# Expert gather that fills a whole PSUM bank before copying it, and larger limits on the ring of expert weights

## The chip, the core and the metric

The kernel runs on one NeuronCore of one Trainium2 chip. The core has a matrix engine (TensorE, "PE" in the profile), three engines for elementwise work (VectorE "DVE", ScalarE "ACT", GpSimd "POOL") and a queue, SyncE ("SP"), which here issues the loads from HBM. Each engine works through its own list of instructions in order and waits on semaphores where it needs something from another. The metric is device time in microseconds for one launch.

## The reference

Two layers over 512 tokens of width 1024, all float32. Each layer adds three things to the residual x:

```python
x = x + merged @ w_out[i]                 # merged = sig(ga) * attention + sig(gb) * convolution
x = x + _hier_moe(_rms_norm(x, norm_ffn[i]), ...)   # top-1 group, top-2 of its 8 experts
x = x + sigmoid(_rms_norm(x) @ W_pg) * (p[i] @ W_pe)
```

There are 32 experts. Each has a gate and an up matrix (1024 x 512) and a down matrix (512 x 1024), and computes `(silu(xb @ w_gate) * (xb @ w_up)) @ w_down` for its tokens. The weights of the experts of one layer are 384 pieces of 512 KB, some 200 MB, and each of them is read from HBM once.

## The kernel before

**Layer.** The first part of a layer, the mixer, projects x, runs attention and convolution, and then works through eight chunks `ao0` to `ao7` (attention and convolution output, 24 matmuls each; the loop that ends at L746) and eight chunks `wo0` to `wo7` (output projection, the routing of tokens woven into its second half). The weights of a mixer chunk arrive raw (L207, 512 KB, issued by SP), ACT rounds them to a high part (L225), POOL makes the low part (L230), and PE multiplies with both.

**MoE.** The second part handles the experts in eight chunks c = 0 to 7 of four experts (two pairs). In each chunk PE goes, in this order, through: gate and up matmuls of both pairs; the down matmuls of the pairs of the chunk before; transposes of the hidden values (`ps_hT`); the gather for the next chunk (`ps_xg`); and the combine of the pairs whose down is ready (`ps_c`, added to x by DVE at L1079). PE's instructions are kept in program order in the MoE.

**Gather.** The tokens of an expert are picked by matmul with a one-hot matrix: for each of eight slices of 128 features there are eight matmuls of 128x256 (four token tiles, high and low part, `gather_part`), and ACT copies the result with a scale (L998) to `s_xg`. A slice fills half of a PSUM bank, and so two slices share one bank, four banks per gather.

**Weights.** `pump` (L241) issues the expert weights in a fixed order through SP into slots of the pool `s4`, 45 tiles of 4 KB per partition, which also holds other large tiles (raw mixer weights, `s_xg`, `s_yh`, x). A call stops when the pool has fewer than `keep` free tiles, or when the ring already holds `limit` weights. The limits `RING` apply in the mixer: RING[0] in the loop over `ao`, RING[1] behind it and in `wo0` to `wo3`, RING[2] in the routing part. In the MoE only `KEEP[c]` counts. SP is one queue in order: a load whose slot isn't free yet holds up all loads behind it. At most eight loads are in flight.

**Around the middle.** At the start of chunk 4 the inputs of the embeddings are loaded (L1109, split by ACT at L1110 and by POOL at L1111), and two raw loads (L207) follow on SP. After chunk 4 stands a loop for experts with too many tokens (L1218). It normally runs zero times, but all engines meet there, and each waits for the loads issued so far.

Of the kernel before, what the change touches and what calls it, by code (L numbers as in the profile page):

```python
# [12 lines left out]
AF = mybir.ActivationFunctionType  # L13
# [14 lines left out]
GS = 256  # L28
# [25 lines left out]
              + [f"wo{i}" for i in range(8)] + ["pe0", "pe1"] + [f"pg{i}" for i in range(8)])  # L54
NCH = len(SEQ_CHUNKS)

RING = 2, 12, 20
KEEP = 6, 10, 6, 6, 8, 10, 12, 8
LAGS = 1, 2, 1, 5
OVC = 4  # L60
# [95 lines left out]
class Trunk:  # L156
# [310 lines left out]
    def mixer(self, l):  # L467
        nc = self.nc
        v, act = nc.vector, nc.scalar
# [254 lines left out]
        for j in range(8):  # L724
            c = pos[f"ao{j}"]
            wh, wl = self.take(c)
            pab = [self.ps.get(F32, "ya"), self.ps.get(F32, "yb")]
            for s, src in ((1, cv), (0, oT)):
                for k in range(4):
                    w = slice((4 * s + k) * P, (4 * s + k + 1) * P)  # L730
                    self.mm3(pab[s], wh[:, w], wl[:, w], src[0](k), src[1](k), k == 0, k == 3)
            self.done(c)
            g = gates.pop(0)
            ga, gb = g[:, :T], g[:, T:]
            act.activation(pab[1], pab[1], AF.Identity, bias=self.smt[:, S_BO + j:S_BO + j + 1])
            v.scalar_tensor_tensor(gb, gb, 1.0, pab[1], op0=OP.add, op1=OP.mult)
            v.scalar_tensor_tensor(pab[0], ga, 1.0, pab[0], op0=OP.add, op1=OP.mult)
            v.tensor_tensor(pab[0], pab[0], gb, op=OP.add)
            for h in range(2):
                a = slice(256 * h, 256 * h + 256)  # L740
                act.activation(mT[0].half(j, h), pab[0][:, a], AF.Copy, scale=0.5)
                v.scalar_tensor_tensor(mT[1].half(j, h), pab[0][:, a], 0.5, mT[0].half(j, h).bitcast(F32),
                                       op0=OP.mult, op1=OP.subtract)
            self.ps.free(2)
            self.s4.free()
            self.pump(RING[0])  # L746
        for s in oT + tuple(cv):
            s.free()
        self.pump(RING[1])


        pacc = [self.ps.get(F32, "wo") for _ in range(NT)]
        for i in range(4):
            self.step_b(pos[f"wo{i}"], pacc, mT, 2 * i, i == 0, i == 3)
            self.pump(RING[1])
        for t in range(NT):
# [9 lines left out]

        def hook():
            self.advance(steps)
            self.pump(RING[2])
        for t in range(NT):  # L770
            steps.append(self.route_tile(t))
            self.half[t] = self.token_b(cs, mT, t, hook)
            if t % 2:
                for s in mT:
                    s.free(t // 2)
# [189 lines left out]
    def moe(self, l):  # L965
        nc = self.nc
        self.nc = Engines(self.tc, ("te",))
        v, act, pe = nc.vector, nc.scalar, self.nc.tensor
        oh = self.oh0
# [12 lines left out]
        def gather(oh, xg, h):  # L982

            scale = lambda k: self.smt[:, S_NF + k:S_NF + k + 1]
            out = lambda k: xg[h // 2][:, (k % 4) * GS:(k % 4 + 1) * GS]
            if self.xg0:
                for k in (2 * h, 2 * h + 1):
                    ps = self.xg0.pop(0)[:, :GS]
                    self.gather_part(ps, oh, k, NT - 1)
                    self.last_a = act.activation(out(k), ps, AF.Copy, scale=scale(k)).ins  # L990
                    self.ps.free()
                return
            ps = self.ps.get(F32, "xg")
            for i in range(2):
                k, w = 2 * h + i, slice(i * GS, (i + 1) * GS)
                for t in range(NT):
                    self.gather_part(ps[:, w], oh, k, t)
                act.activation(out(k), ps[:, w], AF.Copy, scale=scale(k))  # L998
            self.ps.free()

        oht, gs, rh, hT, ys = {}, {}, {}, {}, {}
# [121 lines left out]
        for h in range(4):  # L1123
            gather(oh, xg, h)
        self.s4.free()
        for c in range(NC2):
# [4 lines left out]
            if c < NC2 - 1:  # L1131
                oh = self.onehots(c + 1)
# [19 lines left out]
            if c < NC2 - 1:  # L1152
                xg = [self.s4.get(F32, "xg") for _ in range(2)]
                for h in range(4):
                    gather(oh, xg, h)
                self.s4.free()
                if c == NC2 - 2:
                    self.s4.free(2 * NT)
# [324 lines left out]
```

## Time and profile before

| | us |
|---|---|
| median of 3 runs | 1946.11 (1943.98 to 1948.0) |
| profiled execution | 1943.51 |
| its span | 1941.7 |
| PE busy | 1812.1 (93%) |
| DVE, ACT, POOL busy | 916.9, 565.8, 377.9 |

The granted clock of TensorE was 0.974 of full speed over the span. In the profile a wait is written `[idle before <-releaser]`; `SPq` and `DVEq` are the sequencers of SyncE and VectorE. The section on rows below has what was read.

### The profile page before, as it was taken

The page shows a single profiled execution, that of the slowest core. Times are in us where ns is not written, and L with a number is a line of the kernel's source. Part 1 is how long each engine was busy: PE and PEld are TensorE (multiplying, and loading weights), DVE is VectorE, ACT ScalarE, POOL GpSimd, SP SyncE. Part 2 cuts the span into 40 slices and gives each one's busy share as a digit, 9 for nine tenths or more (in the row PEclk, how much of TensorE's full clock was granted, in tenths as well). Part 3 has the DMA queues.
Part 4 walks back from the last instruction along what each step waited for, and adds up shares of the span by engine and source line. Part 5 has one row for each costly group of instructions (what it writes and reads, how often), then busy time and mean ns, then how long its engine had stood idle before and what let it go on. Part 6 is the DMA issues. An engine that isn't in the chain of part 4 may idle for free. (4 is left out here: it accounts for less than half of the span.)

```text
span 1941.7 us, 23302 instructions
## 1 busy us (share of the span) xinstructions
PE 1812.1 (93%) x8532; PEld 1124.4 (58%) x8532; DVE 916.9 (47%) x2165; ACT 565.8 (29%) x1071; POOL 377.9 (19%) x201
## 2 busy tenths in 40 slices
PE   5999999999999889999989999998999989999987
PEld 4776777753454345354767776877444553454456
DVE  5677754652431332323657777537432423332146
ACT  4444444220111012112634555333110111021045
POOL 3444324201000000000444444241010000000021
PEclk9999999999989999999999999999999999999999
DMA  5211227589999889997231112375898989899941
GB/s 217 83 55 66 65 98 227 189 321 357 349 351 410 343 312 382 388 409 303 81 117 65 61 59 66 127 242 195 308 401 326 381 351 401 349 364 409 409 176 44
DMA packets 133319, 478.59 MB, mean 246 GB/s; under 512 B 14800, under 2 KB 15312, under 8 KB 133200
## 3 DMA queue, kind: packets, MB, share of 16 engines
q1 hardware_dynamic: 133200, 477.04, 65.1%
q8 instruction: 70, 1.15, 0.2%
q14 instruction: 49, 0.40, 0.1%
HBM read 474.89 MB, written 2.10 MB: 246 GB/s over the span
## 5 line engine op out<-in xcount | busy, mean ns | idle before, releaser
L230 POOL TENSOR_TENSOR s_lo<-s_raw,s_hi 128x1024 fp32r<-128x1024 f32 x114 | 272.3, 2400 | 950.5 <-ACT s_hi L225 326.6
L94 PE MATMUL ps_g<-s_w,s_xg 128*64 128x512 f32 x1024 | 230.9, 604 | 4.4 <-DVEq L1218 4.4
L94 PE MATMUL ps_y<-s_w,s_hT 128*64 128x512 f32 x1024 | 225.8, 593 | 0.4 <-DMA s_w<-wdn 0.4
L94 PE MATMUL ps_u<-s_w,s_xg 128*64 128x512 f32 x1024 | 225.2, 592 | 0.0
L290 PE MATMUL ps_z<-s_hTl,s_hi 128*128 128x512 f32 x512 | 204.4, 399 | 0.0
L289 PE MATMUL ps_z<-s_hTh,s_hi 128*128 128x512 f32 x512 | 202.0, 395 | 0.0
L291 PE MATMUL ps_z<-s_hTh,s_lo 128*128 128x512 f32 x512 | 200.4, 391 | 0.0
L94 PE MATMUL ps_xg<-s_OH,s_xh 128*128 128x256 f32 x476 | 138.9, 322 | 59.6 <-ACT s_xg L998 55.8
L1079 DVE TENSOR_TENSOR s_x<-s_x,ps_c 128x512 f32<-128x512 f32 x128 | 87.9, 687 | 155.6 <-PE ps_c L94 132.4
L94 PEld LDWEIGHTS ps_y<-s_w,s_hT 128*64 128x64 f32 x1024 | 74.5, 137 | 148.4 <-issue 136.2
L94 PEld LDWEIGHTS ps_g<-s_w,s_xg 128*64 128x64 f32 x1024 | 73.0, 139 | 149.7 <-issue 142.2
L94 PEld LDWEIGHTS ps_u<-s_w,s_xg 128*64 128x64 f32 x1024 | 73.4, 137 | 146.3 <-issue 141.2
L501 DVE SCALAR_TENSOR_TENSOR s_acc<-ps_z,smt,s_acc 128x511 f32<-128x511 f32 (+27 forms) x210 | 153.7, 732 | 4.2
L94 PEld LDWEIGHTS ps_xg<-s_OH,s_xh 128*128 128x128 f32 x476 | 101.4, 213 | 74.2 <-ACT s_xg L998 68.5
L94 PE MATMUL ps_xg<-s_OH,s_xl 128*128 128x256 f32 x476 | 130.9, 305 | 0.0
L225 ACT ACTIVATE s_hi<-s_raw 128x1024 fp32r<-128x1024 f32 x120 | 124.5, 1055 | 0.7
L1034 ACT ACTIVATE s_h<-ps_g,rs 128x512 f32<-128x512 f32 x32 | 22.0, 687 | 343.1 <-PE ps_g L94 331.8
L1035 DVE SCALAR_TENSOR_TENSOR s_h<-s_h,ps_g 128x512 f32<-128x512 f32 x32 | 22.0, 687 | 188.2 <-ACT s_h L1034 188.2
L290 PEld LDWEIGHTS ps_z<-s_hTl,s_hi 128*128 128x128 f32 x512 | 96.7, 189 | 21.4 <-issue 3.0
L289 PEld LDWEIGHTS ps_z<-s_hTh,s_hi 128*128 128x128 f32 x512 | 96.5, 189 | 21.5 <-issue 1.0
L291 PEld LDWEIGHTS ps_z<-s_hTh,s_lo 128*128 128x128 f32 x512 | 96.5, 189 | 19.1
L1045 ACT ACTIVATE s_hT<-ps_hT 128x512 f32<-128x512 f32 x32 | 17.6, 596 | 304.1 <-PE ps_hT L94 263.2
(256 smaller groups left out, 2873.9 us busy)
## 6 DMA issues: line engine op xcount, KB each, us to landing
s_w<-wu SPq DMA_DIRECT2D x256, 512.0 KB, 10.1
s_w<-wdn SPq DMA_DIRECT2D x256, 512.0 KB, 10.2
s_w<-wg SPq DMA_DIRECT2D x248, 512.0 KB, 10.2
s_raw<-wd SPq DMA_DIRECT2D x124, 512.0 KB, 3.5
s_w<-wg SPq DMA_DIRECT2D x16, 256.0 KB, 7.9
s_x<-x SPq DMA_DIRECT2D x4, 512.0 KB, 9.4
out<-s_n SPq DMA_DIRECT2D x8, 256.0 KB, 2.0
s_gain<-gains SPq DMA_DIRECT2D x3, 512.0 KB, 3.7
```

The source lines that it names most:

```text
L94: i = f(*a, **k)
L225: nc.scalar.activation(hi, raw, AF.Copy)
L230: nc.gpsimd.tensor_tensor(lo, raw, hi.bitcast(F32), op=OP.subtract)
L289: mm(out, lh, rh, start=start, stop=False)
L290: mm(out, lh, rl, start=False, stop=False)
L291: mm(out, ll, rh, start=False, stop=stop)
L501: v.scalar_tensor_tensor(o, i, w, o, op0=OP.mult, op1=OP.add)
L1034: act.activation(t, pg, AF.Tanh, scale=rh[p])
L1035: v.scalar_tensor_tensor(t, t, 1.0, pg, op0=OP.add, op1=OP.mult)
L1045: act.activation(o, ps, AF.Copy)
L1079: v.tensor_add(xs, xs, ps)
```

## The change

In `gather`, the eight matmuls of both halves of a bank are written first, and the two copies after them. Before, each half had its eight matmuls and then its copy. The limits of the ring become 6, 18, 28 in place of 2, 12, 20; in the loop over `ao` the limit now grows by one with each chunk; in the routing part three tiles of the pool are kept free. The kernel has one line more after it, so that lines behind the gather are counted one higher.

```diff
-RING = 2, 12, 20
+RING = 6, 18, 28
...
-            self.pump(RING[0])
+            self.pump(RING[0] + j)
...
-            self.pump(RING[2])
+            self.pump(RING[2], keep=3)
...
             ps = self.ps.get(F32, "xg")
+            half = [ps[:, i * GS:(i + 1) * GS] for i in range(2)]
             for i in range(2):
-                k, w = 2 * h + i, slice(i * GS, (i + 1) * GS)
                 for t in range(NT):
-                    self.gather_part(ps[:, w], oh, k, t)
-                act.activation(out(k), ps[:, w], AF.Copy, scale=scale(k))
+                    self.gather_part(half[i], oh, 2 * h + i, t)
+            for i in range(2):
+                act.activation(out(2 * h + i), half[i], AF.Copy, scale=scale(2 * h + i))
             self.ps.free()
```

**PE, in a gather of layer 0.** `s_OH` is the one-hot matrix, `s_xh` and `s_xl` are the high and low parts of the tokens; the two halves of bank `ps_xg_3551` follow each other. Before:

```order
1609 L94 MATMUL ps_xg_3551<-s_OH_3276,s_xh_2809 128x256 [waits PE_49]
1610 L94 MATMUL ps_xg_3551<-s_OH_3276,s_xl_2810 128x256
...
1616 L94 MATMUL ps_xg_3551<-s_OH_3276,s_xl_3115 128x256
1617 L94 MATMUL ps_xg_3551<-s_OH_3276,s_xh_2809 128x256 [waits Activation_49]
1618 L94 MATMUL ps_xg_3551<-s_OH_3276,s_xl_2810 128x256
```

Now:

```order
1609 L94 MATMUL ps_xg_3551<-s_OH_3276,s_xh_2811 128x256 [waits Activation_49]
1610 L94 MATMUL ps_xg_3551<-s_OH_3276,s_xl_2812 128x256
...
1616 L94 MATMUL ps_xg_3551<-s_OH_3276,s_xl_3115 128x256
1617 L94 MATMUL ps_xg_3551<-s_OH_3276,s_xh_2811 128x256
1618 L94 MATMUL ps_xg_3551<-s_OH_3276,s_xl_2812 128x256
...
1625 L94 MATMUL ps_xg_3570<-s_OH_3276,s_xh_2811 128x256
```

The order of PE's matmuls is the same; the wait on ACT in the middle of the bank is gone, and one on an earlier ACT instruction stands at this bank's start; the next bank, `ps_xg_3570`, starts without a wait.

**ACT, at the start of chunk 4.** L998 (now L999) is the copy of the gather, L1110 (now L1111) the split of the embeddings' input `s_pT`. Before:

```order
312 L998 ACTIVATE s_xg_4686<-ps_xg_4725,smt 128x256 x2
313 L998 ACTIVATE s_xg_4686<-ps_xg_4744,smt 128x256
314 L1110 ACTIVATE s_pTh_4811<-s_pT_4813 128x1024
315 L998 ACTIVATE s_xg_4686<-ps_xg_4744,smt 128x256
316 L1034 ACTIVATE s_h_4904<-ps_g_4838,rs_4895 128x512
```

Now:

```order
312 L999 ACTIVATE s_xg_4686<-ps_xg_4725,smt 128x256 x2
313 L999 ACTIVATE s_xg_4686<-ps_xg_4744,smt 128x256 x2
314 L1111 ACTIVATE s_pTh_4811<-s_pT_4813 128x1024
315 L1035 ACTIVATE s_h_4904<-ps_g_4838,rs_4895 128x512
```

The last copy of the gather no longer stands behind the split of `s_pT`.

**SP, at the loop over `ao`.** `s_raw` are mixer weights, `s_w` expert weights. Before:

```order
52 L241 DMA s_w_2276<-wg 128x1024
53 L241 DMA s_w_2278<-wg 128x1024
54 L207 DMA s_raw_2314<-wd 128x1024
55 L207 DMA s_raw_2354<-wd 128x1024
...
59 L207 DMA s_raw_2514<-wd 128x1024
60 L241 DMA s_w_2550<-wg 128x1024
```

Now:

```order
52 L241 DMA s_w_2276<-wg 128x1024
...
58 L241 DMA s_w_2322<-wu 128x1024
59 L207 DMA s_raw_2324<-wd 128x1024
60 L241 DMA s_w_2360<-wu 128x1024
61 L207 DMA s_raw_2366<-wd 128x1024
62 L241 DMA s_w_2402<-wu 128x1024
63 L207 DMA s_raw_2408<-wd 128x1024
64 L241 DMA s_w_2444<-wu 128x1024
```

Seven expert weights stand ahead of the first of these raw loads where two stood, and then one ahead of each next one. In the MoE the order on SP is the same in both kernels.

**ACT, in the loop over `ao`.** L735 adds the bias, L741 writes the merged tile, L225 is the split of a raw weight. Before:

```order
199 L735 ACTIVATE ps_yb_2281<-ps_yb_2281,smt 128x512
200 L225 ACTIVATE s_hi_2350<-s_raw_2206 128x1024
201 L741 ACTIVATE s_mTh_2234<-ps_ya_2280 128x256
```

Now:

```order
199 L735 ACTIVATE ps_yb_2289<-ps_yb_2289,smt 128x512
200 L741 ACTIVATE s_mTh_2234<-ps_ya_2288 128x256
...
205 L735 ACTIVATE ps_yb_2369<-ps_yb_2369,smt 128x512
206 L225 ACTIVATE s_hi_2362<-s_raw_2206 128x1024
```

The split of raw tile 2206 stands two `ao` chunks later in ACT's order.

## Rows read from the trace of the kernel before

**Rows 1.** The page: busy time by engine; then the rate of the loads in 40 equal slices of the span.

```profile
PE 1812.1 (93%) x8532; PEld 1124.4 (58%) x8532; DVE 916.9 (47%) x2165; ACT 565.8 (29%) x1071; POOL 377.9 (19%) x201
GB/s 217 83 55 66 65 98 227 189 321 357 349 351 410 343 312 382 388 409 303 81 117 65 61 59 66 127 242 195 308 401 326 381 351 401 349 364 409 409 176 44
```

**Rows 2.** The table of waits of PE: who waited for whom, us in total, times, longest.

```profile
PE ps_xg L94 <- ACT s_xg L998: 55.8, 58, 2.5
...
PE ps_c L94 <- ACT s_xg L998: 6.3, 2, 4.9
...
PE ps_g L94 <- DVEq L1218: 4.4, 2, 2.2
...
PE ps_yb L291 <- POOL s_lo L230: 2.0, 2, 1.0
```

**Rows 3.** PE's timeline in the gather at the end of chunk 1, layer 0: start, us, instruction, idle before it. The first bank's second half begins at 488.23, the second bank's at 490.97.

```profile
484.77 0.28 PE L94 MATMUL ps_xg<-s_OH,s_xl 128*128 128x256 f32 x1
...
485.49 0.28 PE L94 MATMUL ps_xg<-s_OH,s_xl 128*128 128x256 f32 x1
488.23 0.39 PE L94 MATMUL ps_xg<-s_OH,s_xh 128*128 128x256 f32 x1 [2.46 <-ACT s_xg L998]
...
490.97 0.39 PE L94 MATMUL ps_xg<-s_OH,s_xh 128*128 128x256 f32 x1 [0.56 <-ACT s_xg L998]
```

**Rows 4.** ACT's timeline in the same stretch.

```profile
485.39 2.43 ACT L1065 ACTIVATE s_yh<-ps_y,gs 128x512 fp32r<-128x512 f32 x4
487.66 0.52 ACT L998 ACTIVATE s_xg<-ps_xg,smt 128x256 f32<-128x256 f32 x1
489.49 0.47 ACT L998 ACTIVATE s_xg<-ps_xg,smt 128x256 f32<-128x256 f32 x1 [1.30 <-PE ps_xg L94]
```

**Rows 5.** Windows cut around the fourteen gathers (seven per layer): stretch, its length, busy time and instructions of each engine, granted clock, share of the DMA engines, GB/s. The last line sums all fourteen.

```profile
431.20:442.50 11.30, 9.04 (x69) 8.09 (x69) 7.41 (x21) 3.94 (x9) 0.00 (x0) 1.00 0.87 344
484.50:497.60 13.10, 8.94 (x68) 8.13 (x67) 8.55 (x21) 6.52 (x13) 0.00 (x0) 1.00 1.03 409
547.00:563.80 16.80, 12.64 (x68) 11.56 (x67) 8.54 (x21) 6.50 (x13) 0.00 (x0) 0.70 1.03 409
...
754.70:767.70 13.00, 8.84 (x68) 8.03 (x67) 3.48 (x6) 8.29 (x15) 2.84 (x2) 1.00 1.03 410
822.60:835.60 13.00, 8.85 (x68) 8.03 (x66) 3.21 (x6) 6.53 (x13) 0.00 (x0) 1.00 1.03 408
1391.70:1402.80 11.10, 8.84 (x67) 7.94 (x65) 7.39 (x21) 3.91 (x8) 0.00 (x0) 1.00 0.87 348
...
1709.70:1722.70 13.00, 8.84 (x68) 8.03 (x67) 3.48 (x6) 8.30 (x15) 2.83 (x2) 1.00 1.03 409
1777.60:1791.90 14.30, 10.15 (x69) 9.33 (x67) 3.21 (x6) 6.54 (x13) 0.00 (x0) 0.88 1.03 410
sum 193.90, PE 139.42 PEld 126.98 DVE 76.33 ACT 89.50 POOL 5.67; mean PE 9.96 PEld 9.07 DVE 5.45 ACT 6.39 POOL 0.40
```

**Rows 6.** Windows with the same columns: from the first gate matmul of chunk 1 to the landing of the last load before the loop, in layer 0 and in layer 1; the first stretch of the former; a stretch of chunks 6 and 7.

```profile
442.40:701.60 259.20, 237.64 (x1164) 116.38 (x1164) 77.98 (x161) 35.22 (x66) 11.67 (x5) 0.95 0.94 365
1402.80:1661.50 258.70, 240.64 (x1184) 119.99 (x1184) 82.06 (x166) 35.23 (x66) 11.68 (x5) 0.96 0.94 366
...
442.50:460.00 17.50, 17.50 (x82) 5.81 (x84) 3.99 (x10) 1.14 (x2) 0.00 (x0) 1.00 0.87 307
...
800.00:900.00 100.00, 94.08 (x455) 46.06 (x450) 25.84 (x47) 14.93 (x27) 0.00 (x0) 0.98 1.03 409
```

**Rows 7.** SP's timeline around the loads of the embeddings, layer 0; nothing is issued between the two rows.

```profile
627.61 0.33 SPq L1109 DMA_DIRECT2D s_pT<-pT  x1
641.23 0.80 SPq L207 DMA_DIRECT2D s_raw<-wd  x2
```

**Rows 8.** SP's table of waits from 442 to 702 us.

```profile
SPq L241 <- PE ps_xg L94: 19.8, 5, 9.3
...
SPq L241 <- PE ps_c L94: 13.3, 4, 6.4
```

**Rows 9.** The first gate matmul behind the loop in layer 0 and in layer 1, the last down matmuls of chunk 5 in layer 0, and the combine of chunk 3, from PE's timeline.

```profile
708.93 3.60 PE L94 MATMUL ps_g<-s_w,s_xg 128*64 128x512 f32 x8 [2.20 <-DVEq L1218]
...
1664.12 4.49 PE L94 MATMUL ps_g<-s_w,s_xg 128*64 128x512 f32 x12 [2.19 <-DVEq L1218]
...
752.06 1.93 PE L94 MATMUL ps_y<-s_w,s_hT 128*64 128x512 f32 x6 [0.21 <-DMA s_w<-wdn]
...
639.17 0.79 PE L94 MATMUL ps_c<-s_yh,s_OHT 128*128 128x512 f32 x1 [4.88 <-ACT s_xg L998]
```

**Rows 10.** ACT's split of the embeddings' input in chunk 4, layer 0, with the wait before it.

```profile
637.70 1.06 ACT L1110 ACTIVATE s_pTh<-s_pT 128x1024 fp32r<-128x1024 f32 x1 [11.05 <-DMA s_pT<-pT]
```

**Rows 11.** The mixer: the groups of the two splits (busy, mean ns, idle before), the issue of six raw loads on SP, one matmul of an `ao` chunk that waited for a split, and the median time of a raw load from issue to landing.

```profile
L225 ACT ACTIVATE s_hi<-s_raw 128x1024 fp32r<-128x1024 f32 x120 | 124.5, 1055 | 0.7
...
L230 POOL TENSOR_TENSOR s_lo<-s_raw,s_hi 128x1024 fp32r<-128x1024 f32 x114 | 272.3, 2400 | 950.5 <-ACT s_hi L225 326.6
...
276.74 21.78 SPq L207 DMA_DIRECT2D s_raw<-wd  x6
...
314.53 0.50 PE L291 MATMUL ps_yb<-s_cv,s_lo 128*128 128x512 f32 x1 [1.01 <-POOL s_lo L230]
...
s_raw<-wd SPq DMA_DIRECT2D x124, 512.0 KB, 3.5
```

## Prediction, made before the changed kernel ran

> **What bounds the kernel now.** I read the page first: PE is busy 93% of the span, and its slack is small [rows 1]. So I went to the table of what PE waits for. One line there outweighs all others of the MoE: `ps_xg` on ACT's copy L998, 55.8 us in 58 waits [rows 2]. The timeline of one gather shows how it arises. The matmuls of one half follow each other every 0.12 us (six steps in 0.72 us), but the second half of a bank starts only when the copy of the first has ended, because both lie in the same bank [rows 3]. From the second half of one bank to that of the next 2.74 us pass, where sixteen matmuls need 16 x 0.12 = 1.92: each later bank loses 0.81 us. The first bank of a gather loses 2.46, as its copy stands in ACT's queue behind four copies of `s_yh` that take 2.43 [rows 3, 4].
>
> The second view is the rate of the loads. Through the MoE it stands between 312 and 409 GB/s [rows 1], and in chunks 6 and 7 it is 409 for 100 us on end [rows 6], and no slice is above 410. Such a stretch cannot be made faster by PE alone. From the start of chunk 1 to the last load ahead of the loop it is 365 and 366 [rows 6]: there the queue has idle time, but only about a tenth. So two limits stand close together, and what the gather gives back must be checked against the loads.
>
> **The gather, PE's side.** The change takes the wait out of the middle of each bank. A gather is then 64 x 0.12 + 0.3 = 8.0 us. The window of one is 13.1 now (11.3 in chunk 0, which has no `s_yh` ahead of it), and more where the granted clock fell, down to 0.70 of full speed in one [rows 5]. All fourteen windows are 193.9 us [rows 5]; 14 x 8.0 = 112; PE alone would gain 81.9 us. Two waits of the combine for the last copy go too, 6.3 [rows 2]: in chunk 4 this copy stands behind the split of the embeddings' input, which itself waited 11.05 us for its load [rows 9, 10]; the order now has the copy ahead of it. The very first gather of a layer has one bank of this kind, 0.8 each.
>
> **The loads' side, chunk 1 to the loop.** In layer 0 this is 259.2 us at 365 GB/s, that is 94.6 MB or 180 loads of 0.524 MB. At 409 GB/s they take 231.3 us; 27.9 us of the queue are idle. In layer 1, 258.7 x 366/409 = 231.5, idle 27.2 [rows 6]. Part of the idle time is SP waiting for slots which the end of a gather or a combine frees, 19.8 and 13.3 us of waits (some covered by the eight loads in flight) [rows 8]; these come earlier when PE does. Part stays. The start in chunk 1 runs at 307 for 17.5 us, a loss of 17.5 x (1 - 307/409) = 4.4 [rows 6]. SP issues nothing for 13.6 us between the embeddings' load and the raw loads [rows 7], and this stop hangs on ACT and POOL after the load, not on PE; eight loads in flight at 1.28 us cover 10.3, so about 3.6 stay. That makes 8.0 at least. At most I add 5.7 for short stops behind each combine, 13.7. I take the middle, 10.9.
>
> So the last load ahead of the loop lands 231.3 + 10.9 = 242.2 us after the start of chunk 1. All engines wait there for the loads issued, and PE goes on 2.2 us later [rows 9]: 244.4. Before it was 708.93 - 442.40 = 266.5, and in layer 1 1664.12 - 1402.80 = 261.3 against 231.5 + 10.9 + 2.2 = 244.6 [rows 6, 9]. The gain is 22.1 and 16.7, in sum 38.8. PE alone would gain more in this stretch: of its 81.9 + 6.3 over both layers, 6.4 lie in chunk 0 and 21.3 behind the loop (both below), which leaves 60.5 against 38.8. PE's surplus becomes a longer wait at the loop or at down weights.
>
> **Chunk 0.** Its loads run into slots that the gather's end frees, so the line of loads moves with PE: 11.3 - 8.0 and 11.1 - 8.0 [rows 5], with 0.8 each for the first gather, 8.0 in both layers together.
>
> **Behind the loop.** SP's order in the MoE is the same in both kernels, so the same loads have landed when the loop is left. Chunk 5 ends as before: its last down matmuls wait for their weights already now [rows 9], so PE cannot be earlier. The gathers at the ends of chunks 5 and 6 then shrink from 13.0 to 8.0 in layer 0, and from 13.0 and 14.3 to 8.0 in layer 1 [rows 5]: 10.0 + 11.3 = 21.3. The loads run at 409 there [rows 6]; they have some lead, and slots come free earlier by the same amount, so I count it whole; the bound below is nothing.
>
> **The ring.** In the mixer's `ao` loop more expert weights go ahead of raw loads. The raw loads were issued from 276.74 in 21.78 us [rows 11], some ten us or more ahead of need; one weight more ahead of each costs 1.28 us of the line. What moves is the split: ACT's split of one raw tile stands two chunks later. An `ao` chunk waited 1.01 us for such a split before, 2.0 in both layers [rows 2, 11]. I count another 1.2 per layer, -2.4; the bounds are +2.0 (that wait goes) and -14 (the next split waits once for a whole load, split and subtraction, 3.5 + 1.06 + 2.4 = 7.0 [rows 11], per layer). The larger stock brings nothing that I can see: no wait of PE for a load stands in the first chunks, and the ring was filled ahead of the MoE in any case.
>
> **Sum.** 38.8 + 8.0 + 21.3 - 2.4 = 65.7. From the profiled execution's 1943.5 that gives 1877.8; the median of the runs is 2.6 above the profiled one, so **1880 us**.
>
> **The rivals.** *PE is the bound throughout* (0.12): the loads follow PE everywhere. Then 81.9 + 6.3 + 1.6 - 2.4 = 87.4 come back, 1943.5 - 87.4 + 2.6 = 1859. For it speaks the 27.9 us of idle queue, against it that 231.3 us of transfer plus any start and stop is more than PE would need. This sum includes the clock: twelve windows at 13.05 and two at 11.2 would be 179 of the 193.9, so 14.9 us are lost clock. The Trainium skill, "TensorE: Matmul & The Clock Gate", section "A second HAM failure mode: psum-queue depth-cycling", says that PE idling briefly between groups of matmuls as it cycles through PSUM banks makes the clock oscillate. By that the 14.9 us go with the pauses; the trace agrees in that the two gathers of chunk 0, whose pauses are short, ran at 1.00 [rows 5].
>
> *The line of loads does not move* (0.10): the gathers' pauses are the time in which the stock is filled, and the loads end when they ended. Then only the loop's surplus wait in layer 0 (708.93 - 701.6 - 2.2 = 5.1), chunk 0's 8.0 and, of the 21.3, between nothing and all remain: 13.1 to 34.4, less 2.4, a middle of 21: 1943.5 - 21 + 2.6 = 1925. The rate decides it. The stretch of 100 us at 409 GB/s [rows 6] speaks against it. The Trainium skill, "DMA: Bandwidth & Descriptors", section "Specifications", gives an HBM limit of about 358 GB/s per core; by it 180 loads would take an estimated 264 us, the line could not move, and this rival would be the forecast. The trace has 409 over 100 us, so the measurement decides against that figure here.
>
> *The pause moves* (0.03): PE waits at the start of each bank for the two copies of the one before. The order shows such a wait on ACT in one bank. Two copies are 0.94 us against the 0.47 of one [rows 4], paid at three or four bank starts instead of four bank middles: 1946 within 4. Against it: the next bank in the order has no wait at its start, so there are free banks.
>
> *Slower* (0.03): raw mixer loads come late behind the weights. Then each of eleven chunks (`ao5` to `ao7`, `wo0` to `wo7`) waits for load and splits, up to 7.0 us [rows 11], 2 x 11 x 7.0 = 153, less the 68.1: 1943.5 + 153 - 68.1 + 2.6 = 2031. It decides from the point where a raw tile lands less than its two splits, 3.5 us, before PE needs it, and it cancels the gain when half of the chunks do. Against it: the six loads before were issued far ahead.
>
> **How the numbers follow.** The forecast has 0.72, with a range of its own of 1866 to 1894: 5.7 us of stops per stretch (twice), -14 for the ring, and a part of the 21.3. With the first rival whole the range begins at 1858; on the other side it ends at 1904, short of the second rival's middle. 0.2% or 3.9 us is about what a measurement of this kernel can tell from no change. Faster by more is the forecast and the first two rivals, 0.94; within it 0.03, slower 0.03.
>
> **What would show it.** Right: the wait of `ps_xg` on the copy falls from 55.8 to nearly nothing; gathers take 8.0 us at granted clock 1.00; the rate from chunk 1 to the loop rises from 365 to about 390 GB/s; PE's wait at the loop grows from 2.2 to several us, or waits of `ps_y` on down weights appear in chunks 3 and 4; chunk 5 still takes 45 us from its first gate matmul to its last down. Wrong: waits of `ps_c` or `ps_xg` on ACT stay; the rate stays near 365 while PE waits for weights; waits on `s_lo` in the mixer pass 5 us per layer.

## The result

The changed kernel takes 1879.39 us (median of 4 runs, 1876.28 to 1883.5), the kernel before 1945.05 in the same comparison. The ratio is 0.9666, with a 95% interval of 0.9639 to 0.9693. 1880 was forecast.

The table of waits of PE in the changed kernel (us in total, times, longest):

```profile
PE ps_g L94 <- DMA s_w<-wg: 11.2, 2, 5.7
...
PE ps_u L94 <- DMA s_w<-wu: 4.9, 8, 1.2
PE ps_yb L291 <- POOL s_lo L230: 3.3, 4, 1.0
...
PE ps_y L94 <- DMA s_w<-wdn: 2.9, 14, 0.2
```

The line that led the MoE before, `ps_xg` on the copy with 55.8 us [rows 2], is gone, and so is that of `ps_c` on the copy. In their place stand three lines on loads of expert weights, 19.0 us together; before, PE's waits on loads were below half a microsecond.

Windows around four gathers of layer 0 (columns as in [rows 5]):

```profile
428.70:436.80 8.10, 8.10 (x69) 7.97 (x69) 7.42 (x21) 3.21 (x9) 0.00 (x0) 1.00 1.02 407
478.70:486.80 8.10, 8.10 (x69) 8.07 (x68) 3.61 (x7) 5.80 (x13) 0.00 (x0) 1.00 1.02 407
...
535.90:544.10 8.20, 8.20 (x70) 8.20 (x69) 3.65 (x7) 5.82 (x12) 0.00 (x0) 1.00 1.02 409
...
662.90:671.10 8.20, 8.20 (x70) 8.16 (x69) 3.56 (x6) 5.90 (x13) 0.00 (x0) 1.00 1.03 409
```

Each is 8.1 to 8.2 us with PE busy throughout, at a granted clock of 1.00. The third took 16.8 us at 0.70 before [rows 5].

Windows from the start of chunk 1 to the last load landed ahead of the loop, in both layers, then chunk 5 of layer 0:

```profile
436.70:681.50 244.80, 237.69 (x1184) 113.51 (x1184) 82.32 (x170) 33.97 (x67) 11.68 (x5) 1.00 0.99 389
1363.10:1608.50 245.40, 237.66 (x1184) 113.46 (x1184) 82.33 (x170) 33.95 (x67) 11.67 (x5) 1.00 0.99 388
...
683.80:729.00 45.20, 44.74 (x193) 14.34 (x194) 10.73 (x28) 1.38 (x2) 0.00 (x0) 0.97 0.99 390
```

The rate rose from 365 to 389 GB/s [rows 6]; chunk 5 takes the 45 us that it took before. In chunks 1 to 3 PE waits for no load (the chunks take 57.3 us each: 436.62, 493.95, 551.28 and 608.61 are their starts and the start of chunk 4). PE's timeline shows where the loads hold it, in chunk 4 and at the loop, where all engines wait for the loads issued so far:

```profile
630.59 3.50 PE L94 MATMUL ps_u<-s_w,s_xg 128*64 128x512 f32 x10 [1.16 <-DMA s_w<-wu]
...
683.84 1.12 PE L94 MATMUL ps_g<-s_w,s_xg 128*64 128x512 f32 x2 [5.57 <-DMA s_w<-wg]
```

And SP's timeline shows the stop at the embeddings' input, which stayed as long as in [rows 7] (609.14 to 622.82, 13.7 us):

```profile
609.14 0.33 SPq L1110 DMA_DIRECT2D s_pT<-pT  x1
622.82 0.80 SPq L207 DMA_DIRECT2D s_raw<-wd  x2
```

By stretches, from the timelines of both executions, the 67.2 us between the spans (1941.7 and 1874.5) lie here:

| stretch | layer 0 | layer 1 |
|---|---|---|
| from the start of the kernel (layer 0) or of chunk 7 of layer 0 (layer 1) to the first `ao` matmul | 2.0 | 1.0 |
| `ao` loop | -1.0 | -0.9 |
| `wo` to the first gate matmul | 1.5 | 1.1 |
| chunk 0 | 3.3 | 3.3 |
| chunk 1 to behind the loop | 19.3 | 13.6 |
| chunks 5 and 6 | 10.3 | 12.2 |
| chunk 7 of layer 1 to the end | | 1.6 |

The first entry, 2.0, is within what executions differ by: in the profiled executions of all the runs below, which do the same work up to there, the first `ao` matmul starts between 277.98 and 280.98 us. The entries of the `ao` loop are not of this kind (e1 and e2 below); the others of 1 to 2 us were not followed.

### The profile page after: what moved, and what is told of

The parts are those of the page before. It is cut to its first block, busy times and chain, and to the rows that moved or that the text cites. A ratio compares the mean times of both kernels' runs of the same rounds, so it can differ in the third digit from the quotient of the medians.

```text
span 1874.5 us, 23312 instructions
## 1 busy us (share of the span) xinstructions
PE 1790.9 (96%) x8532; PEld 1104.1 (59%) x8532; DVE 913.6 (49%) x2165; ACT 562.4 (30%) x1071; POOL 378.1 (20%) x201
## 4 chain that ended last, share of the span: by engine, by line
PE 74%; DMA 10%; DVE 7%; issue 5%; ACT 2%; POOL 1%; SPq 0%; DVEq 0%; POOLq 0%; ACTq 0%
PE ps_g L94 11%; PE ps_u L94 10%; PE ps_y L94 9%; PE ps_z L290 5%; PE ps_z L289 5%; PE ps_z L291 5%; PE ps_xg L94 5%; PE ps_c L94 5%; DMA s_w<-wdn 4%; DMA s_w<-wg 3%; DMA s_w<-wu 2%; PE ps_tb L289 2%; PE ps_tb L290 2%; PE ps_tb L291 2%; PE ps_S L609 2%
## 5 line engine op out<-in xcount | busy, mean ns | idle before, releaser
L94 PE MATMUL ps_g<-s_w,s_xg 128*64 128x512 f32 x1024 | 229.9, 602 | 11.2 <-DMA s_w<-wg 11.2
L94 PE MATMUL ps_y<-s_w,s_hT 128*64 128x512 f32 x1024 | 236.1, 595 | 3.5 <-DMA s_w<-wdn 2.9
L94 PE MATMUL ps_u<-s_w,s_xg 128*64 128x512 f32 x1024 | 231.2, 593 | 5.1 <-DMA s_w<-wu 4.9
L225 ACT ACTIVATE s_hi<-s_raw 128x1024 fp32r<-128x1024 f32 x120 | 125.9, 1058 | 8.8 <-DMA s_raw<-wd 4.5
L94 PE MATMUL ps_xg<-s_OH,s_xh 128*128 128x256 f32 x476 | 117.4, 288 | 3.8 <-DVE s_OH L950 1.9
L94 PE MATMUL ps_xg<-s_OH,s_xl 128*128 128x256 f32 x476 | 115.9, 285 | 0.0
L94 PEld LDWEIGHTS ps_xg<-s_OH,s_xh 128*128 128x128 f32 x476 | 92.2, 194 | 5.7 <-issue 5.7
```

Source lines behind the costliest of these rows:

```text
L94: i = f(*a, **k)
L225: nc.scalar.activation(hi, raw, AF.Copy)
```

## The experiments

The theory, after the result: the whole gain comes from the gather; PE's side of it is some 88 us, and the loads of expert weights, whose line sets the time from chunk 1 to the loop, take back what is missing. The rivals: the ring feeds the faster PE; something other than the loads holds PE in chunk 4.

**The two parts alone (e1, e2).** e1 has the gather of the changed kernel and the old limits, e2 the other way round.

```diff
-RING = 6, 18, 28
+RING = 2, 12, 20
...
-            self.pump(RING[0] + j)
+            self.pump(RING[0])
...
-            self.pump(RING[2], keep=3)
+            self.pump(RING[2])
```

Expected of e1: 

> The gather's part alone, with the ring's limits of before. Theory (the gain comes from the gather, limited by the loads; the ring costs about 1 us per layer in the loop over ao and brings nothing): 1878 us within 3, the ao loop back at 44.8 us from 45.8, chunk 1 to the loop 247 us as in the changed kernel. Rival (the larger stock of weights feeds the faster PE): 1890 or more, with more waits of PE for weights in chunk 4.

Expected of e2: 

> The ring's part alone, with the gather of before. Theory: 1946 us within 3, the ao loop 1 us longer per layer, the MoE unchanged, waits of ps_xg on the copy still 55 us. Rival (the ring matters): 10 us or more away from before.

e1 took 1880.76 us, ratio 0.9668 (0.9644 to 0.9692), e2 1949.61, ratio 1.0012 (0.9992 to 1.0033). From the first `ao` matmul to the first of `wo0` it was 44.8 us in e1 and 45.8 in e2, in the profiled executions. e2 keeps the line of the copy:

```profile
PE ps_xg L94 <- ACT s_xg L998: 55.6, 58, 2.5
```

So the gather does all of it. The ring's cost is seen in the `ao` loop, 1 us per layer; in the time of the kernel it is too small to tell from none. In e1, with the smaller ring, PE's waits for weights behind chunk 4 are nearly those of the changed kernel:

```profile
PE ps_g L94 <- DMA s_w<-wg: 12.1, 2, 6.5
```

**One bank for each half (e3).** The kernel before, with the order of matmuls and copies left alone:

```diff
-            ps = self.ps.get(F32, "xg")
             for i in range(2):
-                k, w = 2 * h + i, slice(i * GS, (i + 1) * GS)
+                k = 2 * h + i
+                ps = self.ps.get(F32, "xg")[:, :GS]
                 for t in range(NT):
-                    self.gather_part(ps[:, w], oh, k, t)
-                act.activation(out(k), ps[:, w], AF.Copy, scale=scale(k))
-            self.ps.free()
+                    self.gather_part(ps, oh, k, t)
+                act.activation(out(k), ps, AF.Copy, scale=scale(k))
+                self.ps.free()
```

Expected: 

> The kernel before with one edit: each half of the gather gets a PSUM bank of its own, and its copy stands behind its own eight matmuls as before. Theory (PE waits because the copy reads the bank that PE wants to write): the wait of ps_xg on the copy goes as in the changed kernel, gathers of 8 us, 1878 us within 4. Rival (what counts is that the copies stand behind all matmuls of the pair): 1945, waits stay.

1882.09 us, ratio 0.9674 (0.9648 to 0.9701); the wait on the copy is gone. A window of one gather there:

```profile
536.00:544.10 8.10, 8.10 (x69) 7.92 (x68) 6.81 (x15) 5.88 (x13) 0.00 (x0) 1.00 1.03 410
```

So the wait came from the bank that copy and matmul shared, not from where the copy stands among the matmuls. Either way of keeping PE's next write out of the bank being read gives the same time.

**SP's stop at the embeddings' input (e4).** The first raw tile was given the slot of `s_pT`, and so SP waited for that load to land, and then for ACT and POOL to finish with it (changed kernel, SP's waits from 440 to 690 us):

```profile
SPq L207 <- DMA s_pT<-pT: 9.8, 1, 9.8
...
SPq L207 <- POOL s_pTl L1112: 3.6, 1, 3.6
```

The split now stands behind the first pair of chunk 4, so that the raw loads get other slots:

```diff
             nc.sync.dma_start(praw, self.dr["pT"][l])
-            act.activation(self.pT[0].t[0], praw, AF.Copy)
-            nc.gpsimd.tensor_tensor(self.pT[1].t[0], praw, self.pT[0].t[0].bitcast(F32), op=OP.subtract)
-            self.s4.free()
+            self.praw = praw
...
                 ts.append(hidden(p, pg, pu))
+                if c == PEC - 1 and p == prs[0]:
+                    split_embeddings()
```

(`split_embeddings` holds the three lines taken out above.)

Expected: 

> The changed kernel, with the split of the embeddings' input moved behind the first pair of chunk 4 and the two raw loads issued right behind its load, so that SP no longer stops for 13.7 us there. Theory (from chunk 1 to the loop the loads set the pace): the queue's idle time of 3.6 us and the ramp behind it go, 4 to 6 us less per layer, 1869 us; PE's waits for weights in chunk 4 get shorter by as much. Rival (PE sets the pace, its waits in chunk 4 have another cause): 1879, no change.

1867.47 us, ratio 0.9602 (0.9576 to 0.9629). SP's timeline has the stop no more, and the windows from chunk 1 to the first gate matmul behind the loop have 397 and 396 GB/s:

```profile
611.62 0.33 SPq L1110 DMA_DIRECT2D s_pT<-pT  x1
612.90 1.62 SPq L207 DMA_DIRECT2D s_raw<-wd  x2
615.47 9.28 SPq L241 DMA_DIRECT2D s_w<-wu  x8
...
666.72 14.83 SPq L241 DMA_DIRECT2D s_w<-wg  x8
```

```profile
438.70:678.70 240.00, 233.38 (x1187) 113.42 (x1186) 81.47 (x171) 33.97 (x67) 11.66 (x5) 1.00 1.01 397
1359.00:1600.30 241.30, 233.08 (x1187) 113.17 (x1186) 81.54 (x171) 33.95 (x67) 11.67 (x5) 0.99 1.00 396
```

The stretch is 240.0 and 241.3 us, where the changed kernel has 683.84 - 436.70 = 247.1 and, by its timeline, 247.6: 7.1 and 6.3 less, where 4 to 6 were expected. PE's work is the same, so the loads set the time there. This kernel computes all that the changed one does, and is the fastest of those that do.

**Fewer loads (e5, e6, e11).** The odd experts' up matrices are not loaded, and their matmuls read the even expert's: PE's work is the same, a sixth of the expert loads is gone. This in the kernel before (e5) and in the changed one (e6, and e11 again):

```diff
-                                   if p or w == "u" or h < 4 - LATE]
+                                   if (p or w == "u" or h < 4 - LATE) and not (w == "u" and e)]
...
     def half_item(self, it, k):
+        if it[1] == "u":
+            it = it[0], "u", it[2] // 2 * 2, it[3]
...
     def item_free(self, it):
+        if it[1] == "u" and it[2] % 2:
+            return
```

Expected of e5: 

> The kernel before without the loads of the up matrices of the odd experts (their matmuls read the even expert's), 40 loads per chunk in place of 48; PE's work is the same. Theory: before, PE rarely waited for loads, so little is gained: chunk 5 in each layer some 3 us, perhaps 3 more at the embeddings' input, 1937 us. Rival (the loads bound the kernel before): 1900 or less.

Expected of e6: 

> The changed kernel, with the same loads left out as in e5. Theory (the loads take back what the gather gives): PE's own pace, 57.3 us per chunk in chunks 1 to 4, 231.4 us from chunk 1 to behind the loop in place of 247, chunk 5 62.9 in place of 66; 38 us less, 1841; the distance to e5 is then what PE alone gains, 90 to 96 us. Rival (the loads don't bind; waits are those of the loop): 1870 or more, the distance to e5 stays at 66.

Expected of e11: 

> The kernel of e6 once more, since two of its four times lay far from the other two: 1842 us within 3, as the profiled execution of e6. If it is above 1850, the two times of 1842 were the odd ones and PE's side of the gain is under 85 us.

e5 took 1931.3 us (1925.3 to 1936.07), six below what was expected. e6 spread from 1842.18 to 3026.34 with a median of 1851.62, and was repeated: e11 has 1842.85 (1842.17 to 1843.32). From chunk 1 to behind the loop, e6's windows:

```profile
437.70:669.30 231.60, 229.40 (x1186) 112.55 (x1186) 81.73 (x170) 34.28 (x67) 12.42 (x5) 1.00 0.88 336
1347.90:1579.40 231.50, 229.34 (x1185) 112.49 (x1184) 79.72 (x170) 34.29 (x67) 11.71 (x5) 1.00 0.87 336
```

With 336 GB/s the loads are not at their limit, and the stretch takes 231.6 us, PE's own pace. All waits of PE on loads are gone from e6's table; at the loop the 2.2 us of before are back:

```profile
PE ps_g L94 <- DVEq L1223: 4.4, 2, 2.2
```

The distance from e5 to e11 is 1931.3 - 1842.9 = 88.4 us, a little under the 90 to 96 that I expected; the runs of e5 spread over 11 us, so some us of it are uncertain. That is the change when loads don't bind. With all loads it is 66. The loads take back some 22.

e5 gains 12.4 us over the kernel before, where 7 were expected. Its table has no longer the wait of `ps_c` on the copy (6.3 us before, [rows 2]), which hung on the load of the embeddings' input [rows 10]; I had counted 3 of it. How the rest divides was not followed. The 6.3 us are thus not in the 88.4. In their place e5's gathers lost more to the clock in its profiled execution: the sums over the fourteen gathers (columns as in [rows 5]) of e5 and of e11 are

```profile
sum 201.10, PE 149.04 PEld 135.72 DVE 75.78 ACT 88.33 POOL 7.64; mean PE 10.65 PEld 9.69 DVE 5.41 ACT 6.31 POOL 0.55
sum 110.80, PE 110.80 PEld 110.52 DVE 59.14 ACT 71.89 POOL 0.00; mean PE 7.91 PEld 7.89 DVE 4.22 ACT 5.13 POOL 0.00
```

where the kernel before has 193.9 [rows 5].

**The loop (e7, e8).** The changed kernel without the loop, and e4 without it:

```diff
-            if c == OVC:
-                self.overflow(l)
```

Expected of e7: 

> The changed kernel without the loop for experts with too many tokens, which runs zero times here; its meeting of all engines goes with it. Theory (the loads bind, and the loop costs them a drained queue and a restart): 4 to 5 us less per layer, 1870 us; PE's waits move into the down matmuls of chunks 4 and 5. Rival (the wait at the loop is PE's own loss): 8 us or more per layer, 1862 or less.

Expected of e8: 

> The edits of e4 and e7 together. Theory (both give idle time of the queue back, and the loads still bind): the two gains add, 1860 us, with 409 GB/s from chunk 1 to chunk 6. Rival (one gain hides the other, PE's pace is reached): no faster than the better of the two by more than 3 us.

e7 took 1872.32 us, ratio 0.9623 (0.9579 to 0.9666); e8 1856.56, ratio 0.9542 (0.9499 to 0.9584). The same stretch in e7, up to the first gate matmul of chunk 5:

```profile
438.20:680.10 241.90, 237.65 (x1187) 113.57 (x1186) 81.83 (x171) 33.85 (x67) 11.67 (x5) 1.00 0.99 388
```

and in e8:

```profile
436.90:671.00 234.10, 233.12 (x1186) 113.38 (x1185) 80.92 (x171) 33.96 (x67) 11.67 (x5) 1.00 1.02 401
```

Against 247.1 the loop gives 5.2, the stop 7.1, and both together 13.0: they add, as for two stops in one line of loads. In the time of the kernel e7 gains 7.1 us, 3.5 per layer where 4 to 5 were expected. The wait of 5.57 us that PE showed at the loop was not PE's loss alone: without the loop, PE waits for down weights oftener (22 times, 14 in the changed kernel), and the down matmuls of chunk 5 take 18.0 us (707.6 to 725.6 in the timeline), 16.1 in the changed kernel (712.87 to 728.93), where 13.9 is PE's own pace, as in chunks 1 to 3.

```profile
PE ps_y L94 <- DMA s_w<-wdn: 4.6, 22, 0.4
```

The rate in e8 is 401, short of the 409 that I expected.

The meeting cost PE its clock as well: behind the wait the granted clock was 0.50, the lower of its two levels (1.2 of 2.4 GHz), in e4 for 5 us after 5.66 us of idle time (first line), while in e7 it was 1.00 at that place (second line). The kernel before has such a stretch too, 0.51 from 709.0 to 711.5.

```profile
679.00:684.00 5.00, 5.00 (x14) 1.36 (x12) 4.33 (x13) 0.00 (x0) 0.00 (x0) 0.50 0.85 274
...
680.00:690.00 10.00, 10.00 (x47) 3.36 (x48) 6.58 (x16) 0.69 (x1) 0.00 (x0) 1.00 1.03 409
```

**The loop elsewhere (e9, e10).** e4 with `OVC = 5`, and with `OVC = 6` and the tokens' tiles freed behind the loop.

Expected of e9: 

> The kernel of e4 with the loop for experts with too many tokens one chunk later, behind chunk 5. Theory (the meeting costs the loads some 5 us wherever they bind): the wait moves from the end of chunk 4 to the end of chunk 5, 1867 us within 4. Rival (the place behind chunk 4 is the bad one, since the raw loads have just delayed the weights): 1862 or less.

Expected of e10: 

> The kernel of e4 with that loop behind chunk 6, the tokens' tiles held that much longer. Theory: only the down weights of chunk 7 come after it, which have more than 5 us of lead in the end, so part of the 5 us per layer comes back: 1857 to 1865 us. Rival (as in e9, the place makes no difference): 1867.

Both are slower than e4: 1876.2 us (ratio 0.965, 0.9624 to 0.9677) and 1875.28 (0.9644, 0.9618 to 0.9671). Theory and rival missed alike. In e9 PE waits at the loop, and then for a split of the embeddings' weights, which now stands behind the loop on ACT:

```profile
740.91 0.79 PE L94 MATMUL ps_pe<-s_hi,s_pTh 128*128 128x512 f32 x1 [6.07 <-ACT s_hi L225]
```

ACT's timeline has the split:

```profile
739.19 2.00 ACT L225 ACTIVATE s_hi<-s_raw 128x1024 fp32r<-128x1024 f32 x2 [10.75 <-DMA s_w<-wu]
```

ACT itself stood at the meeting until 739.19, and was released by a load: of PE's 6.07 us, 4.35 are the meeting and 1.72 the split. In e9, as in e4, the loads come last.

In e10 SP's eight loads around the loop take 20.50 us from first to last:

```profile
780.89 20.50 SPq L241 DMA_DIRECT2D s_w<-wu  x8
```

In e4 the eight around the loop take 14.83 (above), and eight without a stop about 9.3. The stop is 11.2 us in e10 and 5.5 in e4. PE's wait there is 2.13 us in e10 and 5.66 in e4: in e4 the loads come last to the meeting, while in e10 SP waits 9.1 us for its loads to land and then another 3.2 for the other engines, as its waits from 775 to 805 us say:

```profile
SPq L1224 <- DMA s_w<-wu: 9.1, 1, 9.1
...
SPq L1224 <- DVEq L1223: 3.2, 1, 3.2
```

And the lead of chunk 7's loads was not there: the down matmuls in that chunk took 19.6 us in e10 (834.4 to 854.0 in the timeline) and 13.9 in e4. The tokens' tiles, held longer in e10, do not explain it: SP's waits for slots from 798 to 862 us are 1.5 us in all. What failed in the expectation was to count the lead of the very last down weights for those in front of them.

## Why the prediction was right, point by point

- **The gather on PE's side.** 81.9 us were forecast for the fourteen gathers, from 193.9 to 112. The same fourteen in the changed kernel take 110.8, each of them 7.9 or 8.0 us at a granted clock of 1.00:

```profile
sum 110.80, PE 110.80 PEld 110.53 DVE 55.77 ACT 74.31 POOL 0.00; mean PE 7.91 PEld 7.90 DVE 3.98 ACT 5.31 POOL 0.00
```

  That is 83.1 us less, and pauses and lost clock went together, as foreseen. 87.4 was the price if PE bound throughout; e5 and e11 give 88.4. That these two are so close is partly luck: the 87.4 contain the 6.3 of `ps_c`, which the 88.4 can't contain, and what e5's gathers lost to the clock stands in their place.
- **The loads from chunk 1 to the loop.** 244.4 and 244.6 us were forecast, and 247.1 and 247.6 came: a gain of 19.3 and 13.6 in place of 22.1 and 16.7, 32.9 for 38.8. This is the term that was mis-sized. The stretch to the last landing has 244.8 x 389/409 = 232.8 us of transfer where 231.3 were counted, and 12.0 of idle queue where 10.9 were; the other layer 245.4 x 388/409 = 232.8 and 12.6. So of the 2.7 us missing in layer 0, 1.1 are idle time and 1.5 are loads that had to be moved besides. The idle time was in the range given (8.0 to 13.7), at its upper part, but its pieces were not those of the forecast. Cut into six, the stretch of layer 0 reads

```profile
436.70:454.20 17.50, 17.50 (x82) 5.86 (x84) 3.99 (x10) 1.53 (x3) 0.00 (x0) 1.00 0.97 360
454.20:484.00 29.80, 29.80 (x163) 13.79 (x160) 7.63 (x12) 5.67 (x11) 9.31 (x4) 1.00 1.03 410
484.00:500.00 16.00, 16.00 (x83) 10.47 (x84) 10.84 (x24) 1.68 (x4) 0.00 (x0) 1.00 0.91 342
500.00:605.00 105.00, 105.00 (x551) 51.49 (x548) 32.87 (x71) 16.10 (x32) 0.00 (x0) 1.00 1.03 409
605.00:631.00 26.00, 24.84 (x114) 9.70 (x113) 15.07 (x32) 2.32 (x3) 2.36 (x1) 1.00 0.78 294
631.00:681.50 50.50, 44.55 (x200) 22.19 (x198) 11.91 (x21) 6.66 (x14) 0.00 (x0) 1.00 1.02 408
```

  Measured against 409 GB/s, the start lost 2.1 us where 4.4 were counted, one short stop 2.6 where 2.9 were allowed, and the stop at the embeddings' input 7.3 where 3.6 were counted. The start, priced too high, hid more than half of what the stop was priced too low. e4 confirms the size of the stop, 7.1 and 6.3 us. The price of 3.6 was the time that the eight loads in flight don't cover (13.6 - 8 x 1.28 is 3.4, to be exact). A closer look at the changed kernel, where SP issued at 609.14 and then at 622.82, shows what it left out:

```profile
617.00:619.00 2.00, 2.00 (x12) 0.62 (x10) 0.00 (x0) 0.00 (x0) 0.00 (x0) 1.00 0.38 152
619.00:622.80 3.80, 3.80 (x20) 1.25 (x18) 1.84 (x2) 1.64 (x2) 2.36 (x1) 1.00 0.01 2
622.80:625.00 2.20, 2.20 (x14) 0.75 (x12) 2.09 (x7) 0.00 (x0) 0.00 (x0) 1.00 0.53 158
625.00:629.00 4.00, 4.00 (x22) 1.26 (x18) 1.06 (x3) 0.00 (x0) 0.00 (x0) 1.00 0.97 330
```

  The loads in flight ran out sooner than counted, so that 5.0 us were lost before the next issue, and the restart behind it cost another 2.1.
- **Where PE's surplus goes.** A longer wait at the loop (5.57 us for 2.2) and waits for down weights in chunk 4, as foreseen; waits for up weights in chunk 4 too, which were not named, and none in chunk 3. Chunk 5 is unchanged at 45 us.
- **Chunk 0 and behind the loop.** 3.3 per layer for chunk 0, where 3.3 and 3.1 were forecast. Chunks 5 and 6: 10.3 and 12.2 for 10.0 and 11.3, so the loads allowed it whole.
- **The ring.** -1.2 per layer was forecast, and the `ao` loop lost 1.0 and 0.9. e1 and e2 show that it is the ring's: it goes with the old limits and comes with the new ones. The wait on the split, which was to grow by 1.2 per layer, grew by 1.3 in both layers together (`ps_yb`, from 2.0 to 3.3); where the rest of the 1.9 lies was not followed. The larger stock brought nothing (e1).
- **The rest.** The steps sum to 65.7 and the spans differ by 67.2. The mis-sized term (-5.9) was made up by some 2 us at the start of layer 0, where the code is the same, and by small gains elsewhere. So the agreement of 1880 with 1879.39, closer than that of the steps, is luck.
- **The rivals.** *PE is the bound throughout* falls with e6: it needed fewer loads to come true. *The line of loads does not move* falls with the rate: 389 GB/s over 245 us. That is above the figure of about 358 GB/s that the Trainium skill ("DMA: Bandwidth & Descriptors", "Specifications") gives as the limit per core; it has it as half of a stack's 716 GB/s, and this program runs on one core. *The pause moves* and *slower*: no wait of `ps_xg` on ACT is left, and the mixer's waits on `s_lo` are 3.3 us of `ps_yb` and 0.3 of `ps_tb` in all, under the 5 per layer named as the sign.

## What to carry to other kernels

A wait inside a PSUM bank is cheap to remove, by filling the bank before reading it or by using another bank (e1, e3). But price it twice, once on the engine that waits and once on the line of loads that feeds it: in each stretch the smaller gain is what came, here 66 of some 88 us in all, and the difference tells what to look for next (e4 found 12 of it in one queue that stopped for a slot). A queue's stop cost more here than the time that its loads in flight leave uncovered, since it also had to start again (2.1 of 7.3 us).

## What was not expected of the hardware

The stop of SP at the embeddings' input cost 6.3 to 7.1 us per layer (e4), where 13.6 less eight loads of 1.28 leaves 3.4. And the meeting of all engines, which cost 5.2 us in layer 0 behind chunk 4 (e7), came out some 4 us per layer dearer behind chunk 5 or 6 (e9 and e10, 8 to 9 us above e4 over two layers). Part of that is what stands next to it there: in e9 the split of the embeddings' weights (1.72 us of PE's wait), in e10 the 3.2 us that SP waits after its loads have landed. How the rest divides is not shown.
